# A planned two-block transformer kernel: modulation moved beside the heads, later plans in three places, four head norms at once

## The chip, the cores and the metric

The kernel runs on one core of a Trainium2 chip. Its engines are TensorE (PE in the rows; PEld is its weight load), VectorE (DVE), ScalarE (ACT), GpSimd (POOL) and SyncE (SP), whose queue issues the large transfers. The metric is the device time of one execution in microseconds, as the median over runs; a profiled execution adds a trace, whose span is a little shorter than its own device time.

## The reference

256 tokens of width 1024 pass through two residual blocks and then a third block that is modulated by a vector `c`. Cut to what matters:

```
# block 0 ("even"): gated convolution beside 8 heads of a gated delta rule
q, k, v = silu(causal_conv4(x @ w))            # per head, 128 wide
q, k = l2norm(q), l2norm(k);  beta, g = gates(x)
low = tril(kb @ k.T * decay); u, w = solve(I + low, [v*beta, kb*exp(gc)])
o = rms(recurrence(q, k, u, w)) * silu(z);  x = LN(a*x + [y_a, o] @ w_out)
x = x + (p @ w_pl) * sigmoid(x @ w_pl_gate)
# block 1 ("odd"): 16 heads of HGRN2, then the same LN and gate
# block 2: mod = silu(c) @ w_ada + b_ada  -> six vectors of 1024
hn = rms(x)*(1+sc1)+sh1;  y = [fox, mlstm, moba](hn) @ w_out;  x += g1*y
hn = rms(x)*(1+sc2)+sh2;  x += g2 * ffn(hn)
```

In block 2 the queries and keys of 12 of the 16 heads are normalised by their root mean square over 64 columns ("head norm"). `mod` depends on `c` alone, so it can be computed at any time before block 2.

## The kernel before

**Weights.** All large weights come as 140 chunks of 1 MB (16 blocks of 128x128) on SP's queue into three `raw` buffers. Each half of a chunk is split into a rounded part `hi` (a cast on ACT, L206) and the rest `lo` (a subtraction on DVE, L206), with four buffers for each. A block is three matmuls (`hi` with the activations' `hi`, `hi` with their `lo`, `lo` with their `hi`), so a half chunk is 24 matmuls of 256 columns. A `hi` buffer is free again when PE has done the half chunk that it held: the cast of a half follows PE, and the subtraction follows the cast. The order of PE's matmuls is that of the program. The other engines' orders are made by a scheduler, except the splits of late chunks and the modulation's reductions, which keep the program's order.

**Side work.** Everything that is no dense product is written as generators in queues (`Side`). A plan clock, `side.now`, goes on by 0.65 for every two weight blocks, and `yield us` puts the rest of a generator off by that much of the plan. So the numbers below say behind how many dense matmuls on PE a piece of side work stands; they are no measured times.

**The even stage (to about 252 us).** Units run in the order h0 h1 h2 h3 c0 h4 c1 h5 c2 h6 c3 h7 c4 to c7. A head (`h`) is 16 blocks for q and k, 16 for v and z; then causal convolutions of four taps (one ACT product into `t`, three DVE `t<-psd,prm,t`, written t_a, t_b, t_c where they are told apart), a SiLU into `kq` or `kv`, transposes of these on PE (`psm<-cst,kv`, `psm<-cst,kq`), square sums on ACT (`junk`, `ss`), their root on POOL (`rr`), scalings (`cb`). The gates' chain (`gdn_gates`) runs beside h0: a softplus, then `q` and, for pairs of heads, decay matrices from `gm` (DVE) by `psm<-cst,gm` (PE) and an exponential (ACT). After every fourth head a masked inverse (`gdn_inverse`, tiles T, U, MT, X) and the output of these heads are run at a plan time that INVERSE_US sets.

**Modulation.** `mod` (L950 to L971) loads `c` (`cr`, SiLU on ACT) and then, one after the other, 48 tiles `wa` of 0.5 MB; each is one DVE reduction over 1024 columns. `MOD` lists for three calls how many, the plan time between two, and the buffers: 13 in the pool `ln0` (behind the heads), 27 in the odd stage, 8 later.

**Layer norm.** `out_ln_gate` runs the output product, statistics (`BN_STATS`, `rs` on POOL), then x, its split into `yh` and `yl`, and the gate's product. During it the next chunk's split keeps the program's order (`late`).

**Head norms.** `heads` runs three groups of two PSUM banks; `head_norm` squares a bank on ACT, sums it on DVE (`hss`), takes the power on POOL (`hrs`), multiplies on DVE (`sq<-psd,hrs`) and transposes on PE 8.45 later. Its queue `kq` runs two at a time, with two buffers of each tile. A PSUM bank is free after the multiplication; there are four `psd` banks.

Of the kernel before, what the change touches and what calls it, by code (L numbers as in the profile page):

```python
# [23 lines left out]

INVERSE_US = 30.0


MOD = [(13, 4.4, 1), (27, 7.35, 2), (8, 10.0, 2)]
BLK = 16
# [113 lines left out]
class Stream:  # L143


    def __init__(self, net, dram):
        self.net, self.dram, self.n, self.have, self.pos = net, dram, dram.shape[0], {}, 0
        self.late = False
        self.fetch(0)

# [5 lines left out]
    def take(self, width=1):  # L156
        c, b = divmod(self.pos, BLK)
        self.pos += width
        if b == (0 if c else BLK // 2):
            self.late |= c == 0  # L160
            self.fetch(c + 1)
            self.have.pop(c - 1, None)
        hi, lo = self.have[c]
        h, j = divmod(b, BLK // 2)
        s = slice(j * P, (j + width) * P)
        return hi[h][:, s], lo[h][:, s]
# [16 lines left out]
class Net:  # L183
# [140 lines left out]
    def run(self):  # L324
        from contextlib import ExitStack
        nc, tc, a = self.nc, self.tc, self.a
        with ExitStack() as es:
            pool = lambda n, **k: es.enter_context(tc.tile_pool(name=n, bufs=1, **k))
            self.wp, self.pp, self.dp = pool("w"), pool("p", space=PSUM), pool("dr", space=DRAM)
            self.cp = pool("c")  # L330
            self.xp = pool("x")
            self.yp = pool("y")
            es.enter_context(tc.manual_schedule(engines={mybir.EngineType.PE}))
            self.side = Side()
            for q, w in (("s1", 2), ("s2", 2), ("hg", 1), ("ln", 4), ("at", 4), ("ada", 1), ("ls", 1), ("kq", 2), ("gt", 1)):
                self.side.queue(q, w)
            self.setup()
            for st in self.stages:
                getattr(self, st)()
# [39 lines left out]
    def even(self):  # L379
        open_ = lambda n: self.tc.tile_pool(name=n, bufs=1)  # L380
        yh, yl = self.ytiles(16)
        with open_("ev") as self.ep:
            self.hs, self.ydone = {}, set()
            with open_("e1") as self.e1:
# [3 lines left out]
                for kind, i in EVEN_UNITS:  # L388
                    if kind == "h":
                        self.gdn_dense(i, yh[:, 8 + i], yl[:, 8 + i])  # L390
                    else:
                        self.conv_a(i, yh[:, i], yl[:, i])
                self.side.until(lambda: len(self.hs) == GH)
            with open_("ln0") as lp:
                self.mod(lp, *MOD[0])
                self.out_ln_gate(0, (yh, yl), self.ydone, lp)
                self.side.until(lambda: self.modded == self.modn)

# [7 lines left out]
    def gdn_gates(self):  # L406
# [19 lines left out]
        self.stt(v3(g), v3(sp), -1.0, ea.unsqueeze(1).to_broadcast([P, 2, 8]))  # L426
        yield 3.5
        q = self.ps("m")
# [68 lines left out]
    def gdn_head(self, h, kq, kv, zs, yh, yl):  # L497
# [62 lines left out]
        if h % 4 == 3:  # L560
            ti = self.gdn_inverse()
            self.inv = self.side.now + INVERSE_US
            for i in range(h - 3, h + 1):
                self.side.add("s2", self.gdn_out(i, self.hs[i], ti[:, 2 * (i % 4):2 * (i % 4) + 2], self.inv))
# [140 lines left out]
    def out_ln_gate(self, i, y, done, lp):  # L705
# [30 lines left out]
        for j in range(4):  # L736
            b = self.ps()
            self.dense((ph, pl), 2, [(b, 0), (b, T)])
            self.w.late = j == 3
            self.act(pw[j // 2][:, 2 * (j % 2):2 * (j % 2) + 2], b.rearrange("p (m t) -> p m t", m=2), AF.Copy, scale=0.5)  # L740
# [410 lines left out]
    def head_norm(self, g, a_, b, kq):  # L1151
        nc, ep = self.nc, self.ep
        yield from self.wait(lambda: self.gated)
        sq = ep.tile([P, 512], F32, tag="sq", bufs=2, name=self.nm("sq"))
        ss, rs = (ep.tile([P, 8], F32, tag=n, bufs=2, name=self.nm(n)) for n in ("hss", "hrs"))
        v8 = lambda t: t.rearrange("p (h d) -> p h d", d=64)
# [301 lines left out]
```

## Time and profile before

| what | value |
|---|---|
| median of 3 runs | 1011.02 us (1010.65 to 1014.03) |
| the profiled execution: its own time, its span | 1009.7 us, 1007.9 us |
| PE busy | 979.7 us, 97% of the span |
| DVE, ACT, POOL busy | 757.2 us (75%), 555.2 us (55%), 51.2 us (5%) |
| DMA on the queue of the large transfers | 177.71 MB, 49.9% of 16 engines |
| `hi` casts, `lo` subtractions | 280 of each, mean 1047 and 1222 ns |

A busy PE is a PE that has a matmul in flight; what PE loses shows as idle time ahead of a matmul, and the row names what released it. Idle time of DVE or ACT by itself costs nothing.

### The profile page before, as it was taken

The numbers are of one execution on the slowest core, as the hardware profiler recorded it, in microseconds if no ns is written. First come the engines' busy times: TensorE is split into PE (matmuls) and PEld (weight loads), VectorE is DVE, ScalarE is ACT, GpSimd is POOL, SyncE is SP. The second block draws the span as 40 slices with busy tenths as digits, with TensorE's granted clock in tenths as the row PEclk, the third lists the DMA queues.
The fourth block names the chain that finished last, engine by engine and source line by source line (L and its number), as shares of the span: only waits on it lengthen the run. The fifth ranks groups of instructions, "written<-read, shape, count | busy, mean of one in ns | idle before, by whom it ended". The sixth has DMA issues, their size and how long they took to land.

```text
span 1007.9 us, 19087 instructions
## 1 busy us (share of the span) xinstructions
PE 979.7 (97%) x7622; PEld 937.2 (93%) x7622; DVE 757.2 (75%) x1449; ACT 555.2 (55%) x1104; POOL 51.2 (5%) x59
## 2 busy tenths in 40 slices
PE   7999999999999999999999999899999999999998
PEld 5999989999998999998999999898867999999998
DVE  5788767878668978979697996879776787665543
ACT  6765556654544664464545544577566674444431
POOL 1000000000000000000000000000141000000000
PEclk9999999999999999999999999999999999999999
DMA  7445523345555685655556455354523257654560
GB/s 283 144 152 175 171 86 126 130 169 175 218 192 206 227 325 201 219 178 182 190 192 220 169 178 199 126 178 133 194 91 126 104 191 271 218 200 169 183 214 22
DMA packets 34617, 179.52 MB, mean 178 GB/s; under 512 B 7648, under 2 KB 8672, under 8 KB 16608
## 3 DMA queue, kind: packets, MB, share of 16 engines
q1 hardware_dynamic: 34096, 177.71, 49.9%
q8 instruction: 60, 0.98, 0.4%
q10 hardware_dynamic: 432, 0.59, 0.2%
q14 instruction: 29, 0.24, 0.1%
HBM read 176.97 MB, written 1.31 MB: 177 GB/s over the span
## 4 chain that ended last, share of the span: by engine, by line
PE 57%; DVE 7%; issue 4%; ACT 1%; POOL 1%; POOLq 0%; ACTq 0%; DVEq 0%
PE psd L294 49%; PE psm L294 6%; PE psm L297 2%; DVE lo L206 2%; DVE q L304 1%; ACT hi L206 1%; DVE xl L313 1%; DVE mt L313 0%; DVE wa L971 0%; DVE k L304 0%; DVE x L304 0%; DVE at L304 0%; DVE yl L217 0%; POOL hrs L321 0%; DVE lacc L313 0%
## 5 line engine op out<-in xcount | busy, mean ns | idle before, releaser
L206 DVE TENSOR_TENSOR lo<-raw,hi 128x1024 fp32r<-128x1024 f32 x280 | 341.2, 1222 | 132.4 <-ACT hi L206 130.2
L206 ACT CAST hi<-raw 128x1024 fp32r<-128x1024 f32 x280 | 292.9, 1047 | 249.1 <-PE psd L294 236.2
L294 PE MATMUL psd<-xh,hi 128*128 128x256 f32 (+1 forms) x1296 | 375.6, 290 | 0.0
L294 PE MATMUL psd<-xl,hi 128*128 128x256 f32 (+1 forms) x1296 | 366.8, 283 | 0.8 <-DVE xl L313 0.6
L294 PE MATMUL psd<-xh,lo 128*128 128x256 f32 (+1 forms) x1296 | 366.4, 283 | 0.2 <-DVE lo L206 0.2
L294 PEld LDWEIGHTS psd<-xl,hi 128*128 128x128 f32 x1296 | 245.7, 190 | 1.6 <-DVE xl L313 1.2
L294 PEld LDWEIGHTS psd<-xh,hi 128*128 128x128 f32 x1296 | 245.3, 189 | 1.0
L294 PEld LDWEIGHTS psd<-xh,lo 128*128 128x128 f32 x1296 | 245.5, 189 | 0.5 <-DVE lo L206 0.5
L294 PE MATMUL psd<-yh,hi 128*128 128x256 f32 x448 | 131.9, 294 | 3.7 <-ACT yh L216 3.7
L294 PE MATMUL psd<-yl,hi 128*128 128x256 f32 x448 | 127.1, 284 | 1.4 <-DVE yl L217 1.3
L294 PE MATMUL psd<-yh,lo 128*128 128x256 f32 x448 | 127.2, 284 | 0.0
L294 PEld LDWEIGHTS psd<-yh,hi 128*128 128x128 f32 x448 | 85.2, 190 | 5.2 <-ACT yh L216 4.3
L294 PEld LDWEIGHTS psd<-yl,hi 128*128 128x128 f32 x448 | 85.6, 191 | 2.4 <-DVE yl L217 2.4
L294 PEld LDWEIGHTS psd<-yh,lo 128*128 128x128 f32 x448 | 84.9, 189 | 0.1
L294 PE MATMUL psd<-hi,xh 128*128 128x512 f32 x144 | 59.0, 410 | 2.3 <-DVE sq L304 2.1
L971 DVE SCALAR_TENSOR_TENSOR wa<-wa,cr 128x1024 f32<-128x1024 f32 x48 | 58.4, 1218 | 2.8 <-ACT cr L316 1.6
L294 PE MATMUL psd<-hi,xl 128*128 128x512 f32 x144 | 56.9, 395 | 0.0
L294 PE MATMUL psd<-lo,xh 128*128 128x512 f32 x144 | 56.9, 395 | 0.0
L294 PE MATMUL psd<-al,hi 128*128 128x256 f32 x176 | 49.8, 283 | 0.0
L294 PE MATMUL psd<-ah,lo 128*128 128x256 f32 x176 | 49.7, 282 | 0.0
L294 PE MATMUL psd<-ah,hi 128*128 128x256 f32 x176 | 49.3, 280 | 0.0
L313 DVE SCALAR_TENSOR_TENSOR t<-psd,prm,t 128x255 f32<-128x255 f32 (+2 forms) x72 | 34.2, 476 | 3.9 <-ACT t L316 3.1
(330 smaller groups left out, 1381.9 us busy)
## 6 DMA issues: line engine op xcount, KB each, us to landing
raw<-in_w_dram SPq DMA_DIRECT2D x140, 1024.0 KB, 4.8
wa<-in_w_ada_dram SPq DMA_DIRECT2D x48, 512.0 KB, 4.8
cr<-in_c_dram SPq DMA_DIRECT2D x3, 512.0 KB, 6.0
out_dram<-fo SPq DMA_DIRECT2D x3, 256.0 KB, 2.1
cst<-in_cst_dram SPq DMA_DIRECT2D x1, 580.0 KB, 8.4
x<-in_xT_dram ACTq DMA_DIRECT2D x2, 256.0 KB, 4.4
x<-in_xT_dram SPq DMA_DIRECT2D x2, 256.0 KB, 5.0
lev<-in_lev_dram SPq DMA_DIRECT2D x1, 508.0 KB, 5.1
```

Of the source, the lines that this page charges most:

```text
L206: i = [nc.scalar.copy(hi, r), nc.vector.tensor_tensor(lo, r, hi.bitcast(F32), ALU.subtract)]
L294: self.nc.tensor.matmul(out, lhsT, rhs, start=start, stop=stop, skip_group_check=True, **k)
L297: self.nc.tensor.transpose(out, in_, self.c("ident")[:in_.shape[0], :in_.shape[0]])
L304: self.nc.vector.tensor_tensor(out, a, b, op)
L313: self.nc.vector.scalar_tensor_tensor(out, a, s, b, op0, op1)
L971: self.tc.keep_in_program_order(nc.vector.scalar_tensor_tensor(w, w, 1.0, c, ALU.mult, ALU.mult, accum_out=self.md(j)[:, i % 8:i % 8 + 1]))
```

## The change

Seven edits. The first call of `mod` is made after the dense part of h2 and its 13 reductions are planned 11.0 apart beside the heads; the second call's 27 are planned 6.3 apart and not 7.35. The gates put `q` and the decay matrices off by 5.5 and not 3.5. The first inverse is put off by 35 and not 30. During the layer norm's gate the next chunk is fetched at that chunk's block 4 and not at its block 0 (`hold`). The head norms run four at a time with four buffers. The descriptor scratch is set to 2048.

```
-INVERSE_US = 30.0
+INVERSE_US = 35.0, 30.0
-MOD = [(13, 4.4, 1), (27, 7.35, 2), (8, 10.0, 2)]
+MOD = [(13, 11.0, 1), (27, 6.3, 2), (8, 10.0, 2)]
...
+        self.hold = 0
...
-        if b == (0 if c else BLK // 2):
+        if b == (self.hold if c else BLK // 2):
             self.late |= c == 0
             self.fetch(c + 1)
+            self.hold = 0
...
-("kq", 2)
+("kq", 4)
...
                     if kind == "h":
                         self.gdn_dense(i, yh[:, 8 + i], yl[:, 8 + i])
+                        if i == 2:
+                            self.mod(self.e1, *MOD[0])
...
-                self.side.until(lambda: len(self.hs) == GH)
+                self.side.until(lambda: len(self.hs) == GH and self.modded == self.modn)
             with open_("ln0") as lp:
-                self.mod(lp, *MOD[0])
                 self.out_ln_gate(0, (yh, yl), self.ydone, lp)
-                self.side.until(lambda: self.modded == self.modn)
...
-        yield 3.5
+        yield 5.5
         q = self.ps("m")
...
-            self.inv = self.side.now + INVERSE_US
+            self.inv = self.side.now + INVERSE_US[h // 4]
...
-            self.w.late = j == 3
+            if j == 3:
+                self.w.late, self.w.hold = True, 4
...
-        sq = ep.tile([P, 512], F32, tag="sq", bufs=2, name=self.nm("sq"))
-        ss, rs = (ep.tile([P, 8], F32, tag=n, bufs=2, name=self.nm(n)) for n in ("hss", "hrs"))
+        sq = ep.tile([P, 512], F32, tag="sq", bufs=4, name=self.nm("sq"))
+        ss, rs = (ep.tile([P, 8], F32, tag=n, bufs=4, name=self.nm(n)) for n in ("hss", "hrs"))
...
-    nc = _bacc.Bacc("TRN2", target_bir_lowering=False, num_devices=1)
+    nc = _bacc.Bacc("TRN2", target_bir_lowering=False, num_devices=1, dynamic_dma_scratch_size=2048)
```

Counts of instructions are the same on every engine, but for two more table loads on ACT. What changes is the order. The first place is DVE at the gates, behind the last operation of the softplus. Before:

```order
L313 SCALAR_TENSOR_TENSOR gg_g<-sp_r_190,gg_ea 128x16
L206 TENSOR_TENSOR lo_223<-raw_220,hi_222 128x1024
L206 TENSOR_TENSOR lo_227<-raw_220,hi_226 128x1024
L308 TENSOR_SCALAR gm_261<-cst,gg_g 128x128 x2
L308 TENSOR_SCALAR gm_268<-cst,gg_g 128x128 x2
```

With the change:

```order
L315 SCALAR_TENSOR_TENSOR gg_g<-sp_r_190,gg_ea 128x16
L208 TENSOR_TENSOR lo_223<-raw_220,hi_222 128x1024
L208 TENSOR_TENSOR lo_227<-raw_220,hi_226 128x1024
L315 SCALAR_TENSOR_TENSOR t_34_254<-psd_156,prm,t_34_254 128x255
L208 TENSOR_TENSOR lo_269<-raw_266,hi_268 128x1024
L315 SCALAR_TENSOR_TENSOR t_34_254<-psd_156,prm,t_34_254 128x254
L208 TENSOR_TENSOR lo_273<-raw_266,hi_272 128x1024
L315 SCALAR_TENSOR_TENSOR t_34_254<-psd_156,prm,t_34_254 128x253
L310 TENSOR_SCALAR gm_301<-cst,gg_g 128x128 x2
```

Two more subtractions and the three products of h0's first convolution now stand between the softplus and the first `gm`.

The second place is DVE at head h7 (its k convolution is t_455 before and t_464 after; t_461 and t_471 are its v convolution). The last subtraction shown is that of the half chunk whose cast waits for PE 18 matmuls ahead of this head's transposes. Before:

```order
L206 TENSOR_TENSOR lo_2618<-raw_2615,hi_2617 128x1024
L313 SCALAR_TENSOR_TENSOR t_455_2537<-psd_2468,prm,t_455_2537 128x255
L313 SCALAR_TENSOR_TENSOR t_455_2537<-psd_2468,prm,t_455_2537 128x254
L313 SCALAR_TENSOR_TENSOR t_455_2537<-psd_2468,prm,t_455_2537 128x253
L206 TENSOR_TENSOR lo_2622<-raw_2615,hi_2621 128x1024
```

With the change:

```order
L208 TENSOR_TENSOR lo_2651<-raw_2648,hi_2650 128x1024
L315 SCALAR_TENSOR_TENSOR t_463_2561<-psd_2484,prm,t_463_2561 128x253
L208 TENSOR_TENSOR lo_2655<-raw_2648,hi_2654 128x1024
L315 SCALAR_TENSOR_TENSOR t_464_2567<-psd_2484,prm,t_464_2567 128x255
L315 SCALAR_TENSOR_TENSOR t_471_2634<-psd_2485,prm,t_471_2634 128x255
L315 SCALAR_TENSOR_TENSOR t_464_2567<-psd_2484,prm,t_464_2567 128x254
L315 SCALAR_TENSOR_TENSOR t_471_2634<-psd_2485,prm,t_471_2634 128x254
L315 SCALAR_TENSOR_TENSOR t_464_2567<-psd_2484,prm,t_464_2567 128x253
```

The k convolution stood ahead of that subtraction and stands behind it now, in turns with the v convolution; h4 and h5 show the same move, and h1, h2 and h3 do not.

The third place is DVE at the first layer norm, around the last statistics. Before:

```order
L206 TENSOR_TENSOR lo_4104<-raw_4097,hi_4103 128x1024
L971 SCALAR_TENSOR_TENSOR wa_4091,modv<-wa_4091,cr_3270 128x1024
L772 BN_STATS st_3282<-psm_4119 128x6 x2
L780 BN_AGGR mv_4126<-st_3282 128x2 x2
L308 TENSOR_SCALAR rs_4127<-mv_4126 128x2
```

With the change:

```order
L208 TENSOR_TENSOR lo_4116<-raw_4109,hi_4115 128x1024
L775 BN_STATS st_3344<-psm_4131 128x6 x2
L783 BN_AGGR mv_4138<-st_3344 128x2 x2
L310 TENSOR_SCALAR rs_4139<-mv_4138 128x2
```

The reduction that stood ahead of the statistics is gone from there.

## Rows read from the trace of the kernel before

**Rows 1.** The page: busy time, share of the span and instructions of each engine.
```profile
PE 979.7 (97%) x7622; PEld 937.2 (93%) x7622; DVE 757.2 (75%) x1449; ACT 555.2 (55%) x1104; POOL 51.2 (5%) x59
```

**Rows 2.** Busy time by stretch: us, PE, PEld, DVE, ACT, POOL, clock, DMA share, GB/s.
```profile
0.00:40.00 40.00, 32.04 (x237) 28.46 (x238) 23.94 (x57) 27.12 (x49) 3.91 (x13) 1.00 0.61 231
40.00:120.00 80.00, 80.00 (x656) 79.47 (x655) 68.15 (x158) 50.67 (x119) 4.66 (x6) 1.00 0.50 163
120.00:160.00 40.00, 36.23 (x292) 33.86 (x291) 28.52 (x75) 22.33 (x66) 2.40 (x3) 1.00 0.29 105
...
345.00:630.00 285.00, 283.21 (x2188) 273.86 (x2187) 238.95 (x349) 149.29 (x266) 8.05 (x8) 1.00 0.58 206
```

**Rows 3.** Timeline at the gates and h0: start, duration, [idle before, releaser].
```profile
18.98 1.28 ACT L316 ACT_TABLE_LOAD   x1
20.15 0.87 DVE L308 TENSOR_SCALAR gm<-cst,gg_g 128x128 f32<-128x128 f32 x4
20.49 0.49 PE L294 MATMUL psm<-cst,gm 128*128 128x128 f32 x2 [1.68 <-DVE gm L308]
34.62 0.33 PE L297 MATMUL psm<-cst,kv 128*128 128x128 f32 x1 [0.60 <-ACT kv L316]
39.59 0.16 DVE L304 TENSOR_TENSOR cb<-rr,gg_beta 128x2 f32<-128x2 f32 x1 [1.13 <-POOL rr L321]
41.80 0.38 PE L297 MATMUL psm<-cst,cb 128*128 128x128 f32 x2
```

**Rows 4.** Timeline at head h7, DVE, ACT and PE.
```profile
197.36 1.51 DVE L313 SCALAR_TENSOR_TENSOR t<-psd,prm,t 128x255 f32<-128x255 f32 x3
197.97 1.05 ACT L206 CAST hi<-raw 128x1024 fp32r<-128x1024 f32 x1 [0.92 <-PE psd L294]
199.06 1.23 DVE L206 TENSOR_TENSOR lo<-raw,hi 128x1024 fp32r<-128x1024 f32 x1 [0.18 <-ACT hi L206]
199.29 0.41 ACT L316 ACTIVATE kv<-t 128x256 f32<-128x256 f32 x1
200.07 0.27 PE L297 MATMUL psm<-cst,kv 128*128 128x128 f32 x1
```

**Rows 5.** The tile cr: duration ns min/median/max, first and last start us.
```profile
L971 DVE SCALAR_TENSOR_TENSOR wa<-wa,cr x48: 1203/1218/1226, 261.2 to 897.5; 128x1024 f32<-128x1024 f32 x48
L316 ACT ACTIVATE cr<-cr x3: 1057/1059/1060, 259.0 to 805.9; 128x1024 f32<-128x1024 f32 x3
```

**Rows 6.** PE's waits, 120 to 160 us: us in total, times, longest.
```profile
PE psm L294 <- DVE MT L304: 1.1, 1, 1.1
```

**Rows 7.** PE's waits, 250 to 345 us.
```profile
PE psd L294 <- DVE yl L217: 0.8, 2, 0.5
PE psm L297 <- POOL rs L321: 0.8, 1, 0.8
PE psm L294 <- DVE T L623: 0.6, 1, 0.6
```

**Rows 8.** Timeline at the second layer norm.
```profile
636.35 1.22 DVE L971 SCALAR_TENSOR_TENSOR wa<-wa,cr 128x1024 f32<-128x1024 f32 x1
...
641.82 0.65 PE L297 MATMUL psm<-cst,rs 128*128 128x128 f32 x4 [0.72 <-POOL rs L321]
643.10 1.04 ACT L206 CAST hi<-raw 128x1024 fp32r<-128x1024 f32 x1 [2.07 <-PE psd L294]
...
645.49 0.38 PE L294 MATMUL psd<-yh,hi 128*128 128x256 f32 x1 [2.31 <-ACT yh L216]
```

**Rows 9.** Busy time by stretch, as Rows 2, after two waits of PE.
```profile
645.00:652.00 7.00, 6.09 (x36) 5.90 (x37) 5.61 (x10) 5.37 (x11) 0.00 (x0) 0.76 0.43 150
...
730.00:734.00 4.00, 1.90 (x9) 1.27 (x8) 1.75 (x2) 1.04 (x1) 4.00 (x2) 1.00 0.29 123
```

**Rows 10.** Timeline at the head norms, POOL and PE.
```profile
729.91 4.24 POOL L321 TENSOR_TENSOR hrs<-hss,mhalf 128x8 f32<-128x8 f32 x2 [13.68 <-DVE hss L310]
733.42 0.47 PE L294 MATMUL psd<-hi,xh 128*128 128x512 f32 x1 [2.10 <-DVE sq L304]
```

More of the change, by code (lines that the diff above doesn't have):

```diff
@@ L334, in run @@
             self.side = Side()
-            for q, w in (("s1", 2), ("s2", 2), ("hg", 1), ("ln", 4), ("at", 4), ("ada", 1), ("ls", 1), ("kq", 2), ("gt", 1)):
+            for q, w in (("s1", 2), ("s2", 2), ("hg", 1), ("ln", 4), ("at", 4), ("ada", 1), ("ls", 1), ("kq", 4), ("gt", 1)):
                 self.side.queue(q, w)
```

## The prediction

> **What bounds the kernel now.** I read the page first: PE has a matmul in flight for 979.7 of 1007.9 us [rows 1], so nothing can be won but PE's idle time, some 28 us, and whatever moves other work can only pay, or cost, through it. The busy times by stretch show where that idle time lies [rows 2]. In 40 to 120 us, most of the heads, PE is busy for 80.00 of 80.00 us while VectorE is at 68.15: the heads run without a gap, but on a VectorE with 11.9 us to spare. The gates and h0 (0 to 40 us) lose 8.0 us, the start of the program in them; the first inverse (120 to 160 us) loses 3.8 us, the odd stage 1.8 us in 285. PE takes 656 instructions in those 80 us, 0.122 us each: this is how I turn "so many matmuls earlier" into time. For each gap I then read the timeline or the list of waits and asked what is last there, and in the changed program's order what stands ahead of it.
>
> **The change, part by part.** The reductions cost VectorE the same wherever they stand: 13 of 1.22 us and a short read of the sum each, some 17 us [rows 5], taken from the first layer norm and spread over the heads. Their volume fits into the slack. What counts is what each pushes back, because VectorE and ScalarE work strictly through their lists.
>
> Gates. Put off by 2.0 of the plan, PE has 18 more dense matmuls (2.2 us) before the decay matrices, so it comes to them at 18.81 + 2.16 = 20.97. But on VectorE the first `gm` now stands behind two more subtractions and three convolution products. These take about 1.14 us and 0.42 us each in a full queue (1.23 and 0.48 less the overlap that three products in 1.51 us show) [rows 4]. So `gm` starts not at 20.15 but at 20.15 + 2 x 1.14 + 3 x 0.42 = 23.7, and PE, 0.34 us behind it as before, waits 3.1 us where it waited 1.68 [rows 3]: +1.4. The stage itself may grow by 0.3, an estimate: it holds three convolution products as before, but more table loads on ScalarE. The wait of 0.60 us for h0's `kv` [rows 3] goes, because that SiLU is ahead of two casts now: -0.6. Last, `cb` of h0 was ready at 39.96 and PE came for it at 41.80, a margin of 1.8 us [rows 3]; ahead of the sums that it needs now stand a further cast (1.05) [rows 4], the SiLU of `cr` (1.06) [rows 5] and a table load (1.28) [rows 3], 3.4 us, part of it in ScalarE's idle time, while PE comes 1.2 us later: I take +1.0 (0 to 1.6). Together +2.1. If the queue ahead of `gm` were empty in time, 1.68 and 0.60 would go: bounds -2.3 to +4.
>
> The Trainium skill, "ScalarE: Activation LUTs", section "Table sets: the hidden batching unit", gives about 2.7 us for one table load. The load shown here takes 1.28 us [rows 3]; by the page's figure the two added loads would take 2.8 us more and the gates up to that much longer, and the row decides.
>
> h4, h5, h7. At h7 the k convolution (three products, 197.36 to 198.87) stood ahead of the subtraction whose cast waits for PE; kv was ready at 199.70, and PE came for its transposes at 200.07 with no wait [rows 4]. With the change the same subtraction stands ahead of it. That one can't start before its cast is done (199.02), and the cast waits for PE at 197.97, so no slack elsewhere moves it. It ends at 200.29; the k convolution takes turns with the v convolution, so its last product is the fifth: 200.29 + 4 x 0.42 + 0.48 = 202.4; then ScalarE's 0.41 for `kv`: 202.85. PE waits 2.8 us. What pushed it: a reduction of 1.22 us stands within the q convolution, and so the third product of q went behind a subtraction and k behind the next. h4 has the same order with small products of the inverse between: +2.7. h5 has it too, and is followed on VectorE by the inverse's start; there I add one reduction that nothing hides, 2.8 + 1.3 = 4.1. Bounds for each: 0 (if PE frees the `hi` buffers earlier than in this trace) and 1.5 times the value. In h2 and h3 a reduction was added behind `cb` without moving a convolution: 0.
>
> First inverse. Five more units of plan keep its steps from PE's queue until their operands are there. Of the 3.8 us that PE loses in 120 to 160 us [rows 2], the longest the 1.1 us for MT [rows 6], I let all go but 0.9: -2.9 (0 to -3.8). With h5 that is +1.2.
>
> First layer norm. The reduction ahead of the last statistics goes, and with it the 0.8 us for `rs`; another stood ahead of the T that PE waited 0.6 us for; `yl` now stands ahead of the split that held it for 0.5 us, since the next chunk is fetched later [rows 7]. -1.9 (-3.6 to 0).
>
> Odd stage. 27 reductions come closer together; PE loses 1.8 us there in all [rows 2], so the gain is at most that and a convolution pushed back as above would cost as much: 0 (-1 to +1.5).
>
> Second layer norm. A reduction at 636.35 stood ahead of the statistics and leaves, and PE's wait of 0.72 us for `rs` goes with it. In the 2.31 us for `yh` a cast of 1.04 us stood ahead of the multiplication that makes x; fetched later, it stands behind. The operands of x limit that to half: -0.5 [rows 8]. Together -1.2 (-3 to 0).
>
> Head norms. PE waited 2.10 us for a bank, because the third norm was begun only when the first had ended and its power on GpSimd (two in 4.24 us) came last [rows 10]. With four at a time the second pair's squares stand some 9 us earlier on ScalarE: -1.7 (-2.1 to 0).
>
> The later fetch moves no transfer into PE's way (the casts wait for PE, not for `raw` [rows 4, 8]), and the scratch size shows in no order: both 0.
>
> The sum: 2.1 + 2.7 + 1.2 + 2.8 - 1.9 + 0 - 1.2 - 1.7 = +4.0 us. On the profiled execution that is 1009.7 + 4.0 = 1013.7; the median of the runs lies 1.3 us above that execution, so **1015.0 us**.
>
> **The rivals.**
> *The heads don't wait (faster).* If the half-chunk buffers are freed a matmul group earlier than in this trace, the casts start 2 us or more before they did and the three convolutions are in time. For it: PE has no gap in the heads before. Against it: the cast at h7 shows PE as its releaser. It decides where the three waits together fall below 2.5 us. Without any of them (-9.6): 4.0 - 9.6 = -5.6, 1005.4 us.
> *Half of the waits.* If subtraction and products overlap more, or PE comes later to each head because of the one before, the three cost half: 4.0 - 4.8 = -0.8, 1010.2 us.
> *The clock (slower still).* After the 2.31 us for `yh` the granted clock fell to 0.76 for 7 us, that is 1.2 GHz for about half of them, and 1.7 us were lost; after the 2.10 us at the head norms it stayed at 1.00 [rows 9]. My sum keeps one such fall. Three waits of 2.7 to 4.1 us, and 3.1 at the gates, would each cost 1.7 us if the clock fell behind them: for three, +4.0 + 5.1, 1020.1 us. The Trainium skill, "TensorE: Matmul & The Clock Gate", section "What's actually happening", states that the array falls to half rate when PE has been idle; the row at 645 us agrees, the one at 730 us shows that not each wait does it.
>
> **How the numbers follow.** My forecast has 0.45, and alone reaches from 1012 to 1018; the heads without waits 0.20; half of the waits 0.20; the clock 0.15. A measurement of this kernel tells about 0.3%, 3.0 us, from no change. The forecast lies 1 us above that bound, so a third of its chance (0.13) is "same": faster 0.21, same 0.32, slower 0.47. The range takes in the rival on either side but for their ends: 1005 to 1020.
>
> **What would show it.** In the changed profile: a wait of PE of 3 us for `gm` near 24 us; one of 2.5 to 3 us for `kv` at h4 and h7, a longer one at h5; idle time in the stretch of 40 to 120 us where there was none; no wait of PE for MT and none of 2 us for `sq`; a shorter one for `yh` at both layer norms. I would be wrong if the heads' stretch stays full, or if the granted clock falls below 1.00 behind the new waits.

## The result and the profile after

The changed kernel takes 1028.77 us (median of 4 runs, 1028.4 to 1029.48); the kernel before took 1011.07 us beside it (4 runs). The ratio is 1.017, with a 95% interval of 1.015 to 1.019: slower by 17.7 us, where +4.0 us was forecast, and outside the range. The profiled execution took 1028.81 us with a span of 1027.0, so 19.1 us more than the span of before. A ratio here and below compares the runs of both kernels as a whole and is not the quotient of their medians; the two differ by up to 0.3% (b_hold).

The page of the changed kernel, busy time and the row of the granted clock (40 equal slices):

```profile
PE 989.5 (96%) x7622; PEld 944.1 (92%) x7622; DVE 756.5 (74%) x1449; ACT 560.2 (55%) x1106; POOL 51.2 (5%) x59
...
PEclk9999999999999999999999999999969999999999
```

PE has as many instructions as before [rows 1] and yet is busy for 9.8 us more. No matmul was added, so some ran slower; one slice of the clock, near 745 to 770 us, says where most of them are. Busy time by stretch (columns as in [rows 2]):

```profile
0.00:40.00 40.00, 30.63 (x229) 26.74 (x230) 22.10 (x52) 29.93 (x50) 2.88 (x12) 1.00 0.67 252
40.00:120.00 80.00, 77.05 (x616) 76.15 (x615) 70.99 (x170) 47.95 (x118) 5.68 (x7) 0.98 0.53 179
120.00:160.00 40.00, 36.94 (x299) 35.86 (x299) 29.68 (x66) 19.45 (x50) 1.01 (x1) 0.96 0.45 158
...
345.00:630.00 285.00, 282.97 (x2182) 273.31 (x2182) 238.16 (x347) 149.24 (x268) 8.05 (x8) 1.00 0.58 206
...
744.00:747.00 3.00, 0.84 (x4) 0.44 (x4) 2.63 (x9) 0.46 (x2) 0.34 (x1) 0.95 0.00 0
747.00:762.00 15.00, 14.93 (x40) 9.81 (x41) 10.94 (x65) 6.96 (x28) 5.26 (x4) 0.50 0.20 72
762.00:765.00 3.00, 3.00 (x11) 2.31 (x11) 1.23 (x1) 1.04 (x1) 0.00 (x0) 0.71 0.00 0
765.00:768.00 3.00, 3.00 (x17) 2.42 (x15) 1.02 (x1) 1.19 (x2) 0.00 (x0) 1.00 0.00 0
```

The heads' stretch, full before [rows 2], has lost 2.95 us to idle time and has 40 instructions fewer. In 747 to 762 us PE is "busy" throughout, but at a granted clock of 0.50, the lower of its two levels, with 40 instructions in 15 us; from 765 us on it takes 17 in 3 us. That is how a slow clock looks on this page: full busy time, few instructions.

The timeline of PE in the changed kernel, with the idle time ahead of an instruction in brackets:

```profile
19.10 0.39 PE L296 MATMUL psd<-xh,lo 128*128 128x256 f32 x1 [0.48 <-DVE lo L208]
...
23.87 0.49 PE L296 MATMUL psm<-cst,gm 128*128 128x128 f32 x2 [2.23 <-DVE gm L310]
...
43.72 0.41 PE L299 MATMUL psm<-cst,cb 128*128 128x128 f32 x2 [0.74 <-DVE cb L306]
...
101.06 0.28 PE L296 MATMUL psd<-xh,lo 128*128 128x256 f32 x1
103.55 0.33 PE L299 MATMUL psm<-cst,kv 128*128 128x128 f32 x1 [2.21 <-ACT kv L318]
...
106.09 0.42 PE L296 MATMUL psd<-xl,hi 128*128 128x256 f32 x1
...
108.42 0.28 PE L296 MATMUL psd<-xh,hi 128*128 128x256 f32 x1
...
132.69 0.47 PE L299 MATMUL psm<-cst,kv 128*128 128x128 f32 x1 [2.62 <-ACT kv L318]
...
210.07 0.33 PE L299 MATMUL psm<-cst,kv 128*128 128x128 f32 x1 [2.86 <-ACT kv L318]
...
654.83 0.39 PE L296 MATMUL psd<-yh,hi 128*128 128x256 f32 x1 [1.61 <-ACT yh L218]
...
747.07 0.69 PE L299 MATMUL psm<-cst,ag_cs 128*128 128x128 f32 x2 [2.23 <-DVE snm L310]
...
771.01 1.17 PE L299 MATMUL psm<-cst,pr 128*128 128x128 f32 x7 [1.35 <-DVE pr L310]
```

The forecast's waits are all there: `gm`, and `kv` at h4, h5 and h7. The same matmul of 256 columns takes 0.28 us at 101.06, 0.42 at 106.09 and 0.28 again at 108.42: behind the wait for h4's `kv` the clock fell and came back, and so it did behind h5's (0.96 on the mean of 120 to 160 us, above) and behind h7's. The wait of 2.10 us for `sq` [rows 10] is gone. In its place stands one of 2.23 us, at 747 us, that no step of the prediction has. VectorE's timeline shows its origin, and ahead of it the end of h7's two convolutions:

```profile
207.46 2.43 DVE L315 SCALAR_TENSOR_TENSOR t<-psd,prm,t 128x255 f32<-128x255 f32 x6
...
742.40 0.16 DVE L312 TENSOR_SCALAR hss<-hss 128x8 f32<-128x8 f32 x1
744.37 0.69 DVE L306 TENSOR_TENSOR sq<-psd,hrs 128x512 f32<-128x512 f32 x1 [1.81 <-POOL hrs L323]
744.98 1.22 DVE L208 TENSOR_TENSOR lo<-raw,hi 128x1024 fp32r<-128x1024 f32 x1
746.11 0.48 DVE L306 TENSOR_TENSOR bias<-psm,cst 128x128 f32<-128x128 f32 x2
...
746.94 0.14 DVE L310 TENSOR_SCALAR snm<-smx 128x1 f32<-128x1 f32 x1
```

VectorE stands for 1.81 us at a multiplication that wants GpSimd's power, does a subtraction, and only then adds the first softmax pair's bias, which frees a PSUM bank. With four norms at a time the keys of two groups are complete soon after each other (their transposes start at 735.78 and 740.13 us, where 18.6 us lay between them before), so four softmax pairs start in one go and not two: the first head of each pair takes two of the four `psm` banks, and the third pair's transposes (`ag_cs`) have to wait until the first pair's bank is free.

The same instruction of PE in both traces gives the cost of each stretch (`kv` and `cb` are the transposes of these; "statistics" stands for the transposes `psm<-cst,x` ahead of them):

| up to | start before, us | start after, us | later by, us | forecast of the stretch | measured |
|---|---|---|---|---|---|
| second `kv` of h1 (gates, h0) | 47.91 | 49.86 | 1.95 | +2.1 | +1.95 |
| `cb` of h4 | 105.58 | 111.50 | 5.92 | +2.7 | +3.97 |
| end of the wait for `kv` of h7, less the wait | 200.07 | 207.21 | 7.14 | +1.2 | +1.2 |
| `cb` of h7 | 206.49 | 218.01 | 11.52 | +2.8 | +4.4 |
| statistics of the second layer norm | 627.04 | 638.03 | 10.99 | -1.9 and 0 | -0.5 |
| statistics behind it | 663.60 | 673.27 | 9.67 | -1.2 | -1.3 |
| statistics behind the mixer | 806.25 | 825.32 | 19.07 | -1.7 | +9.4 |

PE's idle time makes +2.15, +2.21, +0.75, +2.86, +0.24, -0.40 and +1.47 us of the seven rows. The rest is time in which PE is busy longer with the same work: +1.76 at h4, +1.52 at h7, +7.93 in the mixer.

### The profile page after: what moved, and what is told of

It is laid out like the page before. It is cut to its first block, busy times and chain, and to the rows that moved or that the text cites. A ratio compares the mean times of both kernels' runs of the same rounds, so it can differ in the third digit from the quotient of the medians.

```text
span 1027.0 us, 19084 instructions
## 1 busy us (share of the span) xinstructions
PE 989.5 (96%) x7622; PEld 944.1 (92%) x7622; DVE 756.5 (74%) x1449; ACT 560.2 (55%) x1106; POOL 51.2 (5%) x59
## 5 line engine op out<-in xcount | busy, mean ns | idle before, releaser
L296 PEld LDWEIGHTS psd<-hi,xh 128*128 128x128 f32 x144 | 27.8, 193 | 7.5 <-issue 1.9
```

The lines of the kernel that those rows point to most:

```text
L296: self.nc.tensor.matmul(out, lhsT, rhs, start=start, stop=stop, skip_group_check=True, **k)
```

## The experiments

My theory after the result: the waits cost what the sum says, the clock falls behind them, and the head norms only exchange one wait for others. The rivals: one single edit (the modulation, or the norms) carries all of it; or the thin stretch of the softmax pairs lowers the clock with no wait at all. In the names, `b_` is an edit of the kernel before and `a_` one of the changed kernel.

**b_norms.** The head norms' part alone (lines cut to what changes in them).

```
-("kq", 2)
+("kq", 4)
...
-tag="sq", bufs=2
+tag="sq", bufs=4
...
-tag=n, bufs=2
+tag=n, bufs=4
```

> The kernel before with the four head norms at once alone (queue width 4, four buffers each). By the prediction on record, the wait of 2.1 us for sq goes: about 1009.4 us. By the theory that the changed profile suggests (the norms of all pairs, begun early, move the transposes and with them the softmax pairs together on TensorE, which then waits for snm, runs few dense products and falls to half its clock), this edit alone costs the 9.4 us that the stretch between 738 and 774 us of the changed profile lost: about 1020.5 us, with a granted clock near 0.5 for some 10 us behind 735 us. A rival: the edit is harmless by itself and costs only where the stages ahead had shifted: within 2 us of 1011.

1018.66 us (1016.73 to 1020.79) against 1011.54; ratio 1.0059, 1.0035 to 1.0084. The part that was to bring 1.7 us costs 6.0 by the ratio (3.5 to 8.5), 7.1 by the medians. Its timeline of PE and its busy time by stretch:

```profile
737.26 0.69 PE L297 MATMUL psm<-cst,ag_cs 128*128 128x128 f32 x2 [2.24 <-DVE snm L308]
```

```profile
735.00:738.00 3.00, 0.76 (x4) 0.41 (x3) 3.00 (x15) 0.96 (x4) 0.05 (x1) 0.70 0.31 46
738.00:750.00 12.00, 12.00 (x33) 7.61 (x33) 10.10 (x60) 6.30 (x26) 5.15 (x4) 0.50 0.19 78
750.00:753.00 3.00, 3.00 (x8) 2.39 (x8) 0.02 (x1) 0.44 (x1) 0.00 (x0) 0.50 0.00 0
753.00:756.00 3.00, 3.00 (x13) 2.38 (x13) 1.23 (x1) 0.83 (x2) 0.00 (x0) 0.96 0.00 0
```

The wait for `snm` and the clock of 0.50 come with the norms and need nothing else of the change. Over 15 us at 0.50 the loss is 7.5 us.

**a_nonorms.** The changed kernel with the norms put back to two.

```
-("kq", 4)
+("kq", 2)
...
-tag="sq", bufs=4
+tag="sq", bufs=2
...
-tag=n, bufs=4
+tag=n, bufs=2
```

> The changed kernel with the head norms as before (width 2, two buffers). If the norms cost 9.4 us by themselves: about 1019 us, the clock at 1.00 behind 740 us and a wait of 2.1 us for sq again. If the loss there comes from the other edits: within 2 us of 1028.8.

1026.31 us; ratio 1.0137, 1.0109 to 1.0165. That meets neither expectation. It is only 2.5 us better by the medians, and its interval overlaps that of the changed kernel: the wait for `sq` came back (2.11 us), and in this profile the clock fell behind it to 0.50, where it had stayed at 1.00 in the trace of before [rows 9].

**b_mod.** The modulation's 13 reductions beside the heads, with the scratch size, which makes the room that their tiles need in that pool.

```
+                        if i == 2:
+                            self.mod(self.e1, *MOD[0])
...
-MOD = [(13, 4.4, 1),
+MOD = [(13, 11.0, 1),
```

> The kernel before with the first 13 reductions moved beside the heads at 11.0 alone (with the smaller descriptor scratch, which makes room for their tiles). The order moves the k convolutions of h4, h5 and h7 behind the late subtraction as in the changed kernel. Theory: waits of PE of 2.2, 2.6 and 2.9 us for kv there and 1.5 us more behind each by the clock, about 12 us, less 1 to 2 us at the first layer norm: about 1021 us. The rival that the order is harmless and the later gates and the later inverse made these waits: within 3 us of 1011, no such wait.

1014.92 us (1012.32 to 1019.83) against 1011.54; ratio 1.0027, 1.0009 to 1.0046. PE waits 2.21 us for `kv` at h4 and 2.62 at h7, and no longer for `rs` at the first layer norm. At h5 it waits 0.4 us where 2.6 were expected: there the moved reductions alone make no long wait. At the end of the profile 5.4 us are lost, falls of the clock behind the waits at h4 and h7 among them. The median rose by 3.4 us and not by some 10.

**b_mod8.** The same, with the first reduction 4.0 of the plan later, so that no convolution product moves behind a subtraction.

```
-            yield 4.0
+            yield 8.0
```

> The kernel before with the 13 reductions beside the heads as in b_mod, but the first of them 8.0 of plan after the call and not 4.0. The 13 still run on VectorE between h2 and c7, but the order now leaves every convolution of h4, h5 and h7 ahead of its late subtraction. Theory (the order is the cause): no wait of PE over 1 us for kv at h4, h5 and h7, clock at 1.00 up to 600 us, and without the reductions at the first layer norm 1009 to 1010.5 us. Rival (the volume of 13 reductions on VectorE is the cause): the waits stay, 1014 us or more.

1013.44 us (1010.72 to 1019.06) against 1010.91; ratio 1.0033, 1.0008 to 1.0059. No wait for `kv` at h4, h5 or h7, as the order says: the place in VectorE's list makes those that b_mod shows at h4 and h7. Others came in their stead (1.51 us for T, 1.72 for `o`, and 3.08 in place of 2.31 for `yh` at the second layer norm), so the time lies above the 1009 to 1010.5 expected.

**a_nomod.** The changed kernel with the 13 reductions back in the first layer norm.

```
-MOD = [(13, 11.0, 1),
+MOD = [(13, 4.4, 1),
...
-                        if i == 2:
-                            self.mod(self.e1, *MOD[0])
...
+                self.mod(lp, *MOD[0])
                 self.out_ln_gate(0, (yh, yl), self.ydone, lp)
```

> The changed kernel with the first 13 reductions back in the layer norm at 4.4. Theory: the waits for kv at h4 (2.2), h5 (2.6) and h7 (2.9) go or shrink to the 1.9 and 1.7 that the later inverse alone leaves at h5 and h7, and the falls of the clock behind them go; the gates and the mixer stay as they are: about 1020 us. Rival: the head waits come from the gates and the inverse together: 1027 us or more.

1022.17 us; ratio 1.0096, 1.0065 to 1.0128: 6.6 us better. The wait at h4 is gone, that at h5 is 0.4, that at h7 1.71. At the first layer norm the later fetch now costs 2.05 us of waiting for the held chunk's `hi`, which the changed kernel does not show there.

**b_inv.** The first inverse at 35.

```
-INVERSE_US = 30.0
+INVERSE_US = 35.0, 30.0
```

> The kernel before with the first inverse put off by 35 alone. Theory (the prediction's term): the waits between 120 and 160 us go but for about 1 us, no convolution moves behind its subtraction: about 1008 us. Rival: a later inverse collides with h5 and h6, which have their own VectorE work: 1011 to 1014.

1011.33 us against 1011.54; ratio 1.0007, 0.9985 to 1.003. In the inverse the waits for MT and T go, that for X grows to 0.98, and 1.86 and 1.71 us for `kv` at h5 and h7 come: the rival of this expectation.

**b_hold.** The later fetch at both gates.

```
-        if b == (0 if c else BLK // 2):
+        if b == (self.hold if c else BLK // 2):
...
+                self.w.late, self.w.hold = True, 4
```

> The kernel before with the later fetch at both layer norms alone. Theory: at the second, PE's wait for yh shrinks from 2.3 to 1.8 us or less and the clock no longer falls behind it (1.7 us); two waits of 0.3 and 0.8 us for the held split are new at each layer norm: about 1009.5 to 1010.5 us. Rival: the new waits take all of it: within 0.5 us of the kernel before.

1017.27 us (1010.47 to 1019.59) against 1010.91; ratio 1.0033, 1.0005 to 1.006. The medians lie 6.4 us apart, the ratio says 3.3; both are dearer than expected. At the second layer norm `yh` is waited for 1.61 us and not 2.31, and the 0.72 for `rs` goes, as forecast. At the first, PE waits for the chunk that was held:

```profile
334.70 0.39 PE L296 MATMUL psd<-yh,hi 128*128 128x256 f32 x1 [2.04 <-ACT hi L208]
335.96 0.58 PE L296 MATMUL psd<-yh,lo 128*128 128x256 f32 x1 [0.76 <-DVE lo L208]
```

**n_early.** The kernel before, with the norm's transposes 2.6 of the plan earlier, and still two norms at a time.

```
-        yield 8.45
+        yield 5.85
```

> The kernel before with the head norms two at a time as they were, but their transposes 5.85 of plan behind the power and not 8.45, so that each pair ends and the next begins some 5 us earlier. Theory: the wait of 2.1 us for sq goes without the softmax pairs coming together, so PE has no wait over 1 us there and the clock has nothing to fall behind: about 1009 us, and none of the single runs above 1012.5 that the kernel before shows. Rival (the sparse matmuls of the softmax pairs lower the clock by themselves): runs above 1013 stay as frequent, or the clock falls in the profile between 730 and 760 us without a wait ahead of it.

1014.88 us; ratio 1.0036, 1.0014 to 1.0057. The wait of 2.10 us is split into 0.97, 1.06, 1.11 and 1.40: more in sum, and slower, though the clock of this profile stays at 1.00 behind all four.

**Filling the waits.** To part the clock from the waits, the next kernels put matmuls with zero weights ahead of the instruction that waits. They add zeros to the bank that is open anyway, or write a bank that the next matmul starts anew, so PE is busy while the release comes when it came before.

```
+    def fill(self, n, o=None, x=None, start=False):
+        if o is None:
+            o, x = self.open
+        for _ in range(n):
+            self.mm(o, self.zero, x, start=start, stop=False)
```

**a_fill.** 20 of 256 columns ahead of `gm`, 20, 24 and 26 ahead of `kv` at h4, h5 and h7, and 10 of 512 at the second softmax pair.

```
+                    if (h, e, s) == (0, 0, 0):
+                        self.fill(20)
                     self.mm(o, gm[:, s], self.c("tri"), stop=False)
...
+        self.fill({4: 20, 5: 24, 7: 26}.get(h, 0))
         for s in range(2):
             self.tr(tk[:, s * P:(s + 1) * P], kv[:, 0, s * P:(s + 1) * P])
...
+                if (p_, e) == (1, 0):
+                    self.fill(10)
                 for a_ in range(2):
                     self.tr(t[:, a_ * P:(a_ + 1) * P], self.cs[:, a_, h:h + 1].to_broadcast([P, P]))
```

> The changed kernel with its PE waits filled: matmuls with zero weights, added to the bank that is open anyway, stand ahead of the first gm product (20 of 256 columns), of the kv transposes of h4, h5 and h7 (20, 24, 26) and of the bias transposes of the second softmax pair (10 of 512 columns). The released events come when they came before, so every wait keeps its length and is spent with a busy PE. Theory (the clock falls behind idle PE; the waits cost about 7.6 us at full clock and the falls behind them 11.5): clock 1.00 at 105, 130, 210 and 745 to 765 us, the time 1028.8 - 11.5 = about 1017. Rival (the thin work of the softmax pairs lowers the clock by itself): the fall from 745 to 765 stays (8.2 us lost) and only the three falls at the heads go, 1025. Second rival (the fall is chance and no wait sets it): 1026 to 1029.

1028.75 us; ratio 1.0172, 1.0145 to 1.0199. The median did not move, but in the profile (1027.44 us, the fastest of six runs) the parts did. Busy time by stretch and PE's timeline:

```profile
40.00:120.00 80.00, 79.28 (x648) 78.50 (x648) 70.35 (x167) 48.07 (x117) 5.68 (x7) 1.00 0.53 179
120.00:160.00 40.00, 38.32 (x323) 37.27 (x322) 30.65 (x71) 20.65 (x57) 1.01 (x1) 1.00 0.46 158
```

```profile
101.09 2.49 PE L304 MATMUL psd<-xh,zeror 128*128 128x256 f32 x20
103.46 0.33 PE L313 MATMUL psm<-cst,kv 128*128 128x128 f32 x1
...
748.34 1.64 PE L304 MATMUL psm<-kq 64*128 64x128 f32 x4 [2.24 <-DVE bias L320]
```

At the heads `kv` is met at the same time (103.46 against 103.55) with a busy PE, the clock is 1.00, and 3.0 us are won by h7 (`cb` at 215.04, not 218.01). The mean clock of its six runs is 0.989 to 0.993, that of the changed kernel's four 0.986 or 0.987. So there the falls come from the idle PE. In the mixer the fill failed: it led the scheduler to another order on VectorE, a wait of 2.24 us stood one instruction later, with 0.50 behind it, and of 2.7 us won up to the mixer 1.4 were lost again in it.

**b_norms_fill.** The norms alone, with the same 10 in the mixer.

> The kernel before with the head norms four at a time, and 10 zero matmuls of 512 columns ahead of the bias transposes of the second softmax pair. Without them this edit alone took 1018.7 and lost 8.5 us to the clock from 735 to 755 us. Theory (the forecast of -1.7 us for this edit was right at full clock, and the fall behind the new wait of 2.24 us is what turned it round): clock 1.00 there, 1018.7 - 8.5 = 1010, that is 0 to 2 us under the kernel before. Rival (the thin work lowers the clock whatever stands ahead of it): 1017 to 1019.

1022.76 us; ratio 1.0103, 1.0078 to 1.0129; the wait is 2.25 us, moved as in a_fill. It tells nothing of the clock.

**b_fill.** Fills in the three long waits of the kernel before: 15 at `gm`, 21 at `yh`, 9 of 512 columns for `sq`.

```
+            if ms is GATE_GROUPS[0]:
+                self.lead = (0, 21)[i]
...
+            self.tail = 9 if g == 1 else 0
             self.dense_tok(self.xs(), KT, b)
```

> The kernel before with zero matmuls in its three long waits: 15 of 256 columns ahead of the first gm product, 21 ahead of the second layer norm's gate product, 9 of 512 columns ahead of the last product of the second group of heads. Theory (the spread of this kernel's runs, 1007 to 1016, is the falls that come behind these waits in some executions): median about 1008, no run above 1011. Rival (the spread has another cause): median 1011 and the same spread.

1018.21 us; ratio 1.0061, 1.004 to 1.0082. Two of the three were badly placed: that at the layer norm read `yh` itself and so waited for it, and that for `sq` stood one group of heads too early and was 2.1 us of work on top. No test of the theory.

**c1.** Modulation as in b_mod8, fetch at block 2, four norms, and fills at `gm` (15) and in the mixer (10).

```
+                self.w.late, self.w.hold = True, 2
...
-            yield 4.0
+            yield 8.0
```

> Modulation beside the heads with its first reduction 4.0 later than in the change (which kept the convolutions ahead of the subtractions), the fetch of the layer norm's gate at block 2, head norms four at a time, and zero matmuls ahead of the first gm product (15 of 256 columns) and of the second softmax pair (10 of 512). Theory: at full clock the parts are worth -2.2 (modulation), some -2 (fetch) and -2.2 (norms) against 1005.8, and nothing falls in the mixer: 1002 to 1006. Rival (falls come back behind other waits, at 128, 154 and 645 us, or in the mixer): 1009 to 1013.

1020.95 us; ratio 1.0085, 1.0061 to 1.0108. Falls behind 1.51 us for T and 1.71 for `o`, and in the mixer behind 2.25 us.

**a_fill4.** a_fill with 4 in the mixer and not 10, which keeps VectorE's order.

```
-                    self.fill(10)
+                    self.fill(4)
```

> As a_fill, but with 4 zero matmuls of 512 columns and not 10 ahead of the second softmax pair, so that VectorE keeps the order of the changed kernel there; some 1.3 us of that wait stay open. Theory (a wait of about 2 us of idle PE is what the clock falls behind, one of 1.3 us is short enough): no fall at the heads and none from 745 to 765 us, 1028.8 - 3.0 (the heads, as a_fill showed) - about 7 = 1018 to 1020. Rival (the thin work lowers the clock, or 1.3 us suffice for the fall): the mixer as in the changed kernel, 1025 to 1026.

1024.6 us (1023.55 to 1024.87); ratio 1.0117, 1.0092 to 1.0141: between the two expectations. The heads' falls are gone, 1.26 us of the mixer's wait are left, and the clock fell to 0.50 behind those; in this profile it also fell behind the 1.61 us for `yh`, where it had stayed at 1.00 in the changed kernel's.

**b_norms_fill4.** The norms alone with those 4.

> The kernel before with the head norms four at a time and 4 zero matmuls of 512 columns ahead of the second softmax pair, VectorE's order as in the run with the norms alone (1018.7). Theory (fall behind the wait): 1010 to 1012. Rival (thin work): 1017 to 1019.

1019.14 us; ratio 1.0065, 1.0043 to 1.0087. The same: 1.26 us of wait, and 0.50 behind it. A shorter wait was not enough.

**a_fill5.** a_fill4 with 6 more, ahead of the first pair's second head.

```
+                self.fill({(0, 1): 6, (1, 0): 4}.get((p_, e), 0))
```

> As a_fill4, with 6 more zero matmuls of 512 columns ahead of the second head's bias transposes of the first softmax pair: 10 in all, VectorE's order that of the changed kernel, and the wait of 2.23 us filled whole (at most 0.2 left). Theory (idle PE): no fall in the mixer, 1024.6 - 6 to 7 = about 1018. Rival (thin work): the fall from 744 to 760 us stays, 1024 to 1026.

1025.6 us; ratio 1.0147, 1.0122 to 1.0172. The 6 stand behind the wait and not in it: the transposes that wait are the third pair's, which come ahead of the first pair's second head. The run shows something else, though not which of the two it is. PE's timeline, and busy time by stretch:

```profile
744.49 0.43 PE L313 MATMUL psm<-cst,ag_cs 128*128 128x128 f32 x2 [1.27 <-DVE snm L324]
...
748.77 2.76 PE L304 MATMUL psd<-xh,zeror 128*128 128x512 f32 x6
...
755.25 0.45 PE L313 MATMUL psm<-cst,ag_cs 128*128 128x128 f32 x2 [1.12 <-DVE snm L324]
```

```profile
747.00:750.00 3.00, 3.00 (x7) 2.15 (x7) 2.47 (x14) 1.59 (x6) 0.00 (x0) 0.50 0.22 93
750.00:753.00 3.00, 3.00 (x12) 1.89 (x10) 0.49 (x4) 0.87 (x3) 0.42 (x1) 0.65 0.00 0
753.00:756.00 3.00, 1.73 (x9) 0.90 (x8) 2.92 (x16) 0.66 (x3) 1.32 (x2) 0.92 0.00 0
756.00:762.00 6.00, 6.00 (x16) 4.49 (x17) 2.67 (x14) 2.60 (x9) 2.36 (x2) 0.50 0.02 4
```

With the fills the clock came back before 756 us, and behind the next wait, of 1.12 us, it fell to 0.50 again. But there the small matmuls go on again too, so this run alone does not tell the wait from the kind of work.

**b_fill2.** The kernel before with 14 zero matmuls at `gm`, 20 at `yh`, and 9 of 512 columns ahead of the third group of heads.

```
+                self.lead, self.leadx = (0, 20)[i], ph[:, 0]
...
+            if g == 2:
+                self.fill(9, self.ps("m"), self.xs()[0][:, 0:2, :T], True)
             b = [self.ps(), self.ps()]
```

> The kernel before with its three long waits really filled: 14 zero matmuls of 256 columns ahead of the first gm product, 20 ahead of the second layer norm's gate, and 9 of 512 columns into a spare bank ahead of the third group of heads; VectorE's order is that of before. Theory (the spread of before, 1009 to 1016 in the last comparison, is falls behind these waits): waits as busy PE, clock 1.00 at 20, 645 and 735 us, median 1007 to 1009, none above 1012. Rival (another cause): 1011 with the same spread.

1011.63 us (1008.93 to 1015.81) against 1011.36; ratio 0.9999, 0.9974 to 1.0024. `gm` and `yh` are filled; the 9 were again one group too early, so one long wait is left, and the runs stand at two levels. Each run's time and mean clock:

```
clock 1.00          1008.93 1009.01 1009.20 1009.48 1009.49 1009.57
clock 0.993, 0.995  1013.70 1015.13 1015.29 1015.30 1015.43 1015.81
```

The profiled one is of the second kind (busy time by stretch):

```profile
732.00:735.00 3.00, 1.70 (x9) 1.27 (x9) 1.63 (x3) 0.05 (x1) 2.03 (x2) 1.00 0.00 0
735.00:738.00 3.00, 3.00 (x9) 1.66 (x8) 2.71 (x14) 1.02 (x4) 0.00 (x0) 0.51 0.33 68
738.00:747.00 9.00, 9.00 (x24) 5.88 (x24) 3.87 (x27) 3.51 (x12) 1.18 (x1) 0.50 0.23 96
```

The same program loses 6 us in half of its executions; in the profiled one it loses them behind the 2.10 us for `sq`.

**b_fill3.** b_fill2 with the 9 at the end of the third group of heads, so that PE comes 2.1 us later to that wait.

```
+            self.tail = 9 if g == 2 else 0
             self.dense_tok(self.xs(), KT, b)
```

> The kernel before with its waits for gm (14 of 256 columns), yh (20 of 256) and sq (9 of 512, at the end of the third group of heads, where PE then comes to the wait 2.1 us later) filled. Theory (idle PE): one level of runs at 1007 to 1008 and the clock at 1.00 throughout the mixer, against 1009 and 1015 in b_fill2 (which carried 2.1 us of fill at a place without a wait). Rival (thin work): runs again at two levels, 1007 and 1013.

1006.69 us (1006.1 to 1007.59, 12 runs) against 1011.19 (1008.64 to 1016.19); ratio 0.9953, 0.9938 to 0.9967. One level, a mean clock of 0.999 or 1.0 in every run, and faster than both kernels. PE's timeline and busy time by stretch:

```profile
641.03 2.51 PE L302 MATMUL psd<-ph,zeror 128*128 128x256 f32 x20
...
728.21 2.28 PE L302 MATMUL psd<-xh,zeror 128*128 128x512 f32 x9
731.48 0.38 PE L311 MATMUL psm<-cst,ag_cs 128*128 128x128 f32 x2
```

```profile
729.00:732.00 3.00, 3.00 (x14) 2.01 (x13) 1.22 (x2) 0.46 (x1) 2.44 (x2) 1.00 0.00 0
732.00:735.00 3.00, 3.00 (x16) 1.80 (x15) 2.85 (x14) 0.91 (x4) 0.00 (x0) 1.00 0.25 52
735.00:744.00 9.00, 9.00 (x47) 6.98 (x47) 7.74 (x37) 6.90 (x23) 1.21 (x1) 1.00 0.25 103
```

The softmax pairs are the same work, 47 instructions in 9 us at 1.00 against 24 in 9 us at 0.50. So in the kernel before the small matmuls do not lower the clock by themselves.

**c4.** The kernel before with the fetch at block 2 and the fills of b_fill2 (14 and not 20 at `yh`).

```
+                self.w.late, self.w.hold = True, 2
...
+                self.lead, self.leadx = (0, 14)[i], ph[:, 0]
```

> The kernel before with the fetch at the gates at block 2 (not 0, and not 4 as in the change), and its three long waits filled as in b_fill2. Theory: the layer norms give 1.5 to 3.4 us and no fall takes them back, 1005 to 1007. Rival (falls behind the waits that the later fetch makes at 333 us, or a spread that the fills do not touch): 1009 to 1014.

1015.99 us; ratio 1.0024, 1.0004 to 1.0045. The wait for the held `hi` is 2.05 us as with block 4: a fetch two blocks earlier does not take that wait away, with the modulation there. In this profile the clock fell behind that wait and behind the 2.10 us for `sq`, which is open here as in b_fill2, so the median is no price of the fetch alone.

## Why the prediction was wrong

The direction was right, the size was not: +4.0 forecast, +19.1 in the profile. Of the difference of 15.1 us the step on the head norms made 11.1, the falls of the clock at h4 and h7 about 2.9, and the first layer norm with the odd stage 1.4. Two mistakes stand behind that: the sum let no new wait be followed by a fall of the clock, and the head norms' step did not follow what is ready next.

**"At h7 ... +2.8", "h4 ... +2.7".** Right as waits (2.86 and 2.21 us), each made by the order that the text names: b_mod8 moves the products back and the waits go. At h7 the step overlooked a second maker, the later inverse, which alone brings 1.71 us (b_inv); the two do not add up. The 0.42 us for a product was misread, since the three products in 1.51 us [rows 4] start 0.52 apart; it held because, taking turns, six take 2.43 us in the changed kernel. What the sum put at nothing is the fall behind each, with which PE is busy 1.76 and 1.52 us longer. Together with the waits that is +3.97 and +4.4. Filling the waits won back 3.0 us.

**"My sum keeps one such fall."** This is the step that failed in general. The rival *the clock* put three falls at 1.7 us each at the heads and gave it 0.15. It had the mechanism, though not the place that counts: it priced a fall at the 1.7 us of dense work, and in the mixer the rows show 15 us at 0.50 and 3 at 0.71, 7.5 + 0.9 = 8.4 us of full-clock work in one fall. The row at 730 us [rows 9] had been read as "behind this wait the clock stays"; a_nonorms and b_fill2 show that it was one outcome of two. The one profile of before held a fall of 1.7 us behind `yh`; its runs of 1014 to 1016 us have a mean clock of 0.991 or 0.992, those near 1009 one of 0.997 or 0.998 (comparison of b_fill3), so they held falls that this trace did not show.

**"Head norms ... -1.7."** Wrong in its sign. The wait for `sq` did go, 2.10 us. What the step left out is who comes next: with two groups' keys ready at once the softmax pairs queue for four `psm` banks behind VectorE's wait for GpSimd, 2.23 us, and 1.35 us more for `pr`. That is 3.58 - 2.10 = +1.5 at full clock, and 8.4 for the fall behind it: 9.9, where 9.4 was measured. The 9.4 is against a trace without a fall behind `sq`; since the kernel before has one in some of its runs, the part costs less between medians, 6.0 to 7.1 us (b_norms).

**Gates, +2.1.** Measured +1.95, in part by luck. The wait for `gm` is 2.23 and not 3.1 (0.55 more than before), `cb` costs 0.74 and not 1.0, and the 0.60 for `kv` is gone: together +0.7. A wait of 0.48 us for `lo` at 19.10 us, which no step has, comes with the later gates (all runs that keep them show it). Some 0.9 us more were waited in the first 13 us, mostly for the first chunk's split; these waits differ from run to run of kernels that start alike (0.2 us for its `hi` and `lo` before, 1.6 in b_inv).

**h5 and first inverse, +1.2.** Measured +1.2, but by luck. The wait for `kv` at h5 is 2.62 us and not 4.1, and a fall of 1.7 us behind it, which the step does not have, makes up the rest. The other waits of the stretch shrank from 3.85 to 1.98 us, 1.9 of the 2.9 forecast; what the remaining 1.2 are stays open. Nor does the named order alone make the wait: it is 0.4 us in b_mod and 1.86 in b_inv. Alone, the inverse's edit is worth nothing (b_inv).

**First layer norm, -1.9.** With the odd stage -0.5. The 0.8 for `rs` went, but the wait for T grew from 0.6 to 0.96; overlooked was that a chunk fetched later is also split later, and PE then waits for its `hi` and `lo` (0.32 and 0.76 us in the changed kernel, 2.04 and 0.76 in b_hold). **Second layer norm, -1.2:** measured -1.3, also by luck. The 0.72 for `rs` is gone and the wait for `yh` is 1.61, but `hi` and `lo` cost 0.3 and 0.8 there too, so the waits give only 0.4; and the fall behind `yh`, which the sum kept, did not come in this trace.

**Scratch size, 0.** It costs nothing that a run shows; the tiles beside the heads need the room.

The Trainium skill, "TensorE: Matmul & The Clock Gate", section "A second HAM failure mode: psum-queue depth-cycling", tells of a kernel that cycles through PSUM banks and whose clock swings between its two levels because PE often idles briefly between groups of matmuls. The mixer of the changed kernel agrees with it in part: it shows one wait of 2.23 us for a bank and 15 us at 0.50 behind it. That could have been a rival of the head norms' step.

Still open: whether the changed kernel's mixer would keep its clock if its wait were filled whole. The fills there left 1.26 and 1.27 us or moved the wait, and the clock fell each time. That the fall there comes from the wait is therefore carried over from the heads (a_fill) and from the kernel before (b_fill3), and not shown in place.

## What to carry to other kernels

Price an idle PE not by its length alone: a wait of 2 us is followed in some executions by a fall that costs 1.5 to 3.4 us in dense work and 5 to 8.5 us in a stretch of small matmuls (in the profiles here), so look at the spread of the runs and at the clock of several profiles before a wait is called harmless. Where a pool or queue is widened, follow what is then ready at the same time, and count the banks that it needs next. If a latency can't be taken away, harmless matmuls in the wait may be worth more than moving the wait elsewhere.

## What the runs showed that I had not expected

Zero-weight matmuls made the kernel before faster: 9 of 512 and 34 of 256 columns are work on top, and the median fell by 4.5 us. Nearly all of it is the clock: where it stayed at 1.00 with one wait left open and 2.1 us of misplaced fill, 1009 us; filled in place, 1006.69.

The spread of this kernel's runs (1008.64 to 1016.19 us) is mostly these falls: it shrinks to 1.5 us once the three waits are filled.

In the twenty profiles of this case each fall of the clock between the first 15 us and the end of the program begins in or shortly behind a wait of PE, the shortest of them 1.08 us. Not each wait does it, and length alone doesn't decide. The 2.31 us for `yh` were followed by a fall in all eight profiles that have them, the 2.10 for `sq` in six of nine, the 1.35 for `pr` in none of nine. In the profiles here 1.12 and 1.26 us in the softmax stretch were followed by 0.50, and 1.35 us for `pr` there, 20 us later, by 1.00; 2.10 us for `sq` by either.
